# Layer 1 attention of a two-layer MoE transformer: first loads, norms, and the turning of attention outputs rearranged

## The chip, the cores and the metric

The kernel runs on one core of a Trainium2 chip. The metric is device time in microseconds (us) of one execution; lower is better. The time of the kernel before is the median of three runs. A profile is one further execution, taken by the hardware profiler; its times count from the start of its span.

## The reference, cut to what matters

A two-layer transformer works on 1024 image tokens and 256 context tokens of width 1024. Each layer normalises its tokens (RMS norm, then scale and shift from a conditioning vector), attends, projects back, adds the result, normalises again, routes every token to 2 of 32 experts and adds the experts' outputs. Layer 1 is sliding-window attention with 16 heads of 64, 4 key/value heads, and a "sink" logit per head:

```python
h = _modulate(_rmsnorm(x, norm1_g[i]), sh1, sc1)
hc = _modulate(_rmsnorm(xc, norm1_g[i]), shc1, scc1)
...
q, k = _rope(q, cos, sin), _rope(k, cos, sin)
...
p = softmax(concat([q k / sqrt(d) + mask, sink]))[..., :-1]
o = p v
x = x + g1 * (o @ w_o)
```

The RMS norm is `x * rsqrt(mean(x*x) + 1e-6)`. Before layer 1, its input is the sum of layer 0's residual and of the two weighted expert outputs of each token, times a gate row (`g2`).

## The kernel before, in words

Everything is float32 in precision: an operand of a large matmul is split into a high and a low part, and two or three matmuls make one product. The stages follow one another: attention 0, projection and routing of layer 0, 32 experts, attention 1, projection and routing of layer 1, 32 experts, a last norm.

Tokens come in 10 tiles of 128: tiles 0 to 7 are the image, 8 and 9 the context. `attention1` (from L1377) takes them in the order 8, 9, 0, 1, ... and has a generator `tick` (L1457) that runs four things for four tiles at once: `combine` of a tile (L1345, ScalarE scales one expert row; L1346, VectorE adds the other; L1348, times `g2`, on VectorE for the first four tiles and on GpSimd for the rest; L1349 adds the residual), `norm1_a` of the tile before (L280: squares with a row sum on ScalarE, `rsqrt`, then the scaled copy L287 on VectorE), `norm1_b` of the tile before that (L290: eight transposes on TensorE, L298; scale and shift of the first four 128-column pieces on ScalarE, L304, of the last four on VectorE, L306; L308 and L309 split into high and low), and the loads of a later tile. `combine_load` (L1341) loads two expert rows per token (`c_y`, L1329) and, for tiles that are not there already, the residual (`c_x`, L1336). `c_y` has four buffers, so the fifth `c_y` load waits until `combine` has released one.

`rsqrt` (L261) is one helper for every norm of the kernel: 10 norms at the start of attention 0, 10 with eight columns (L772) and 18 with one column (L845) in the two projection stages, 10 in attention 1, 8 in the last norm. It computes `v = ss*scale + eps` on VectorE (L268, or L270 where `add` is given), the root on ScalarE (L271), the reciprocal (L272) and one Newton step in four VectorE operations (L273 to L276).

The main loop has four groups of heads. In step `s` of a group it projects the next tile (`qkv`, L337), rotates and transposes queries and keys (L1425, L1432), makes scores (L1539, L1540), and exponentials (L1546 on VectorE, L1555 on ScalarE), and turns the probabilities (L1493) to multiply them with the values (L1504, L1505). A value tile holds high parts in columns 0 to 63 and low parts in columns 64 to 127, so `oT` holds, for 4 heads x 128 queries, 64 rows from the high parts and 64 from the low. `last` (L1510) ends one block (one of 4 groups, one of 8 query tiles; 32 in all): four matmuls (L1515) with a 128x64 matrix `I2`, two stacked identities, turn the block and add its two halves; VectorE multiplies by the reciprocal sums (L1517); ScalarE's queue issues the store (L1518).

```python
pt = ps_t.tile([P, 4, P], F32, name="tr")
for i in range(4):
    nc.tensor.matmul(pt[:, i, 0:64], st["ot"][:, i * P:(i + 1) * P], I2, start=True, stop=True)
oc = pl.tile([P, 4, 64], F32, name="oc", bufs=2)
nc.vector.tensor_tensor(oc, pt[:, :, 0:64], bc(rr, 64, 2), op=OP.mult)
...
```

All transposes and these matmuls write to one ring of two PSUM buffers (`tr`). Every engine and every queue works its instructions in order; which order that is, the framework's scheduler settles when the kernel is built, from the program's order and from what it expects to be ready. So the order in a trace can differ from the text (the small `sink` load stands ahead of the second half of a tile's `c_y` loads, for example). During groups 0 to 2 a second generator, `gen_mods` (L203), makes the conditioning rows of layer 1 with ScalarE (L224) and GpSimd (L225 to L230) beside the rest.

Of the kernel before, what the change touches and what calls it, by code (L numbers as in the profile page):

```python
# [17 lines left out]
OP = mybir.AluOpType  # L18
# [76 lines left out]
class Kernel:  # L95
# [165 lines left out]
    def rsqrt(self, ss, scale, pool, add=None):  # L261

        nc = self.nc
        n = ss.shape[1]
        w = pool.tile([P, 4, n], F32, name=f"rsq{n}", bufs=2)
        v, r, t = w[:, 0, :], w[:, 1, :], w[:, 2, :]
        if add is None:
            nc.vector.tensor_scalar(v, ss, scale, EPS, op0=OP.mult, op1=OP.add)  # L268
        else:
            nc.vector.scalar_tensor_tensor(v, ss, scale, add, op0=OP.mult, op1=OP.add)  # L270
        nc.scalar.activation(t, v, AF.Sqrt)  # L271
        nc.vector.reciprocal(r, t)  # L272
        nc.vector.tensor_tensor(t, r, r, op=OP.mult)  # L273
        nc.vector.tensor_tensor(t, t, v, op=OP.mult)  # L274
        nc.vector.tensor_scalar(t, t, -0.5, 1.5, op0=OP.mult, op1=OP.add)  # L275
        nc.vector.tensor_tensor(w[:, 3, :], r, t, op=OP.mult)  # L276
        return w[:, 3, :]


    def norm1_a(self, xt, pool):  # L280

        nc = self.nc
        xn = pool.tile([P, D], F32, name="n1_xn", bufs=2)
        ss = pool.tile([P, 1], F32, name="n1_ss", bufs=2)
        nc.scalar.activation(xn, xt, AF.Square, accum_out=ss)
        rs = self.rsqrt(ss, 1.0 / D, pool)
        nc.vector.tensor_scalar(xn, xt, rs, None, op0=OP.mult)  # L287
        return xn

    def norm1_b(self, l, t, xn, pool, trp, hT):  # L290

        nc = self.nc
        v = 0 if t < NX else 1
        for half in range(2):
# [5 lines left out]
            for q in range(4):  # L300
                k = half * 4 + q
                a, b = self.Acol[l][:, k, v:v + 1], self.Bcol[l][:, k, v:v + 1]
                if half == 0:
                    nc.scalar.activation(hf[:, q, :], pt[:, q, :], AF.Identity, bias=b, scale=a)  # L304
# [1066 lines left out]
    def attention1(self, es_wo, es_raw, es_o, es2):  # L1371
# [5 lines left out]
        with ExitStack() as es:  # L1377
# [21 lines left out]
            mask = mask.rearrange("p a b -> p (a b)")  # L1399
            I2 = pk.tile([P, 64], F32, name="I2")  # L1400
            nc.vector.tensor_tensor(I2, self.ident[:, 0:64], self.ident[:, 64:P], op=OP.add)

# [42 lines left out]
            work = [[8, 9, 0]] + [[t] for t in range(1, NX)]  # L1445
            g2 = lambda v: self.row_tile(pre, f"g2_{v}", self.mods[0][v:v + 1, 5 * D:6 * D], tag="g2", bufs=2)
            g2 = {1: g2(1), 0: g2(0)}
            prep_w(0)
            while parts:
                parts.popleft()()  # L1450
            ld = {t: self.combine_load(0, t, pre, 2) for t in order[:3]}
            sk = self.row_tile(pk, "sink", A["b_sink"].rearrange("(o d) -> o d", o=1))
# [5 lines left out]
            def tick(i):  # L1458
# [8 lines left out]
                if 0 <= i + 2 < NT:  # L1467
                    xn[order[i + 2]] = self.norm1_a(xs.pop(order[i + 2]), pre)
                yield
                if 0 <= i + 1 < NT:  # L1470
                    t = order[i + 1]
                    hTn[t] = (pa, pre)[(i + 1) % 3 // 2].tile([P, 2, KC, P], F32R, name="hT", bufs=2 - (i + 1) % 3 // 2)
                    self.norm1_b(1, t, xn.pop(t), pre, ps_t, hTn[t])
                yield
# [10 lines left out]
            def av(g, b, E, rr, keys):  # L1485
# [24 lines left out]
                def last():  # L1510
# [3 lines left out]
                    for i in range(4):  # L1514
                        nc.tensor.matmul(pt[:, i, 0:64], st["ot"][:, i * P:(i + 1) * P], I2, start=True, stop=True)  # L1515
                    oc = pl.tile([P, 4, 64], F32, name="oc", bufs=2)
                    nc.vector.tensor_tensor(oc, pt[:, :, 0:64], bc(rr, 64, 2), op=OP.mult)  # L1517
                    getattr(nc, STQ['os1']).dma_start(self.os[b * P:(b + 1) * P, g * 256:(g + 1) * 256].rearrange(  # L1518
# [241 lines left out]
```

## Time and profile before

| | |
|---|---|
| median of 3 runs (lowest, highest) | 3034.24 us (3033.3, 3034.73) |
| the profiled execution, time | 3037.21 us |
| the profiled execution, span | 3035.4 us |
| mean granted clock of TensorE | 0.961 of full speed |

The span is divided as the trace's windows divide it: attention 0 up to about 900 us, projection 0 to about 1085, experts 0 to about 1673, attention 1 to about 2300 (its last steps share time with projection 1, to about 2400), experts 1 to 2987, the last norm to the end. A row of the window view gives the busy time of each engine in a stretch; a row of a line or of a tile gives how often an instruction ran and its shortest, median and longest time in ns; a timeline row gives a start, a length, and in brackets how long the engine was idle before and what released it.

### The profile page before, as it was taken

To read this page: it belongs to the slowest core of one execution; us is meant where nothing else is said; L and a number is where in the kernel's file an instruction comes from. 1 tells how busy PE (TensorE), PEld (TensorE's weight loads), DVE (VectorE), ACT (ScalarE), POOL (GpSimd) and SP (SyncE) were. 2 spreads that over 40 slices of the span, in tenths; PEclk is the share of its full clock that TensorE was granted. 3 is DMA by queue.
4 is the path that set the end of the run, shared out by engine and by line. 5 is a ranking of instruction groups with operands and counts; after the bars stand their busy time and mean duration, and the time that the engine had idled before them with its cause. 6 is when DMAs were issued, how large, how long until landed. Compare 5 with 4: busy or idle time off the path is not lost. (4 is left out here: it accounts for less than half of the span.)

```text
span 3035.4 us, 44263 instructions
## 1 busy us (share of the span) xinstructions
PE 2783.7 (92%) x15206; PEld 2349.0 (77%) x15206; DVE 2422.0 (80%) x4162; ACT 2096.9 (69%) x3725; POOL 1052.7 (35%) x887
## 2 busy tenths in 40 slices
PE   7999999999979979999999489998999799999992
PEld 3888888888857768888888478887888677777772
DVE  4778777777778879989998686665666699999997
ACT  5777777777753258888888487876553478888783
POOL 4756665665521111111110344655100133333330
PEclk8999999999989989999999699999999899999996
DMA  7644554444325479999999745444236799999996
GB/s 259 232 165 165 176 176 161 166 163 157 128 103 202 138 275 377 380 379 377 377 376 352 276 167 180 162 145 153 94 105 212 255 347 365 373 371 368 336 368 265
DMA packets 303214, 745.52 MB, mean 246 GB/s; under 512 B 24612, under 2 KB 80520, under 8 KB 287624
## 3 DMA queue, kind: packets, MB, share of 16 engines
q1 hardware_dynamic: 265032, 680.72, 62.6%
q0 software_dynamic: 19584, 41.98, 3.7%
q10 hardware_dynamic: 18368, 19.93, 1.9%
q8 instruction: 122, 2.00, 0.3%
q14 instruction: 108, 0.88, 0.1%
HBM read 680.60 MB, written 91.29 MB: 254 GB/s over the span
## 5 line engine op out<-in xcount | busy, mean ns | idle before, releaser
L1092 DVE TENSOR_TENSOR elo<-wr,ehi 128x1024 fp32r<-128x1024 f32 x768 | 948.6, 1288 | 62.2 <-ACT ehi L1090 62.2
L1090 ACT ACTIVATE ehi<-wr 128x1024 fp32r<-128x1024 f32 x768 | 762.8, 1061 | 3.3 <-PE y L1158 1.5
L337 PE MATMUL qkv<-w_hi,hT 128*128 128x384 f32 (+1 forms) x1920 | 543.8, 351 | 14.6 <-ACT hT L308 4.9
L337 PEld LDWEIGHTS qkv<-w_hi,hT 128*128 128x128 f32 x1920 | 353.2, 196 | 32.4 <-issue 14.4
L337 PE MATMUL qkv<-w_lo,hT 128*128 128x384 f32 (+1 forms) x960 | 334.3, 348 | 0.0
L1158 PE MATMUL y<-ehi,hidT 128*128 128x512 f32 x1024 | 317.8, 392 | 4.2 <-DVE yb L1169 3.0
L1144 PE MATMUL pg<-ehi,xT 128*128 128x512 f32 x1024 | 291.9, 407 | 3.3 <-ACT ehi L1090 3.3
L1144 PE MATMUL pu<-ehi,xT 128*128 128x512 f32 x1024 | 281.0, 396 | 0.0
L1119 POOL DMA_INDIRECT y_s<-yb,dI x64 | 77.2, 1206 | 513.8 <-ACT yb L1171 482.7
L586 DVE TENSOR_SCALAR_CACHE_REDUCE E<-S 128x1280 f32<-128x1280 f32 (+1 forms) x160 | 203.5, 1272 | 60.8 <-PE S L603 58.8
L1158 PEld LDWEIGHTS y<-ehi,hidT 128*128 128x128 f32 x1024 | 192.5, 188 | 45.7 <-issue 3.4
L594 ACT ACTIVATE E<-E,mx 128x1280 f32<-128x1280 f32 (+1 forms) x160 | 190.9, 1193 | 49.0 <-DVE E L586 48.3
L1173 POOL TENSOR_TENSOR yb<-yb,g 128x1024 f32<-128x1024 f32 x30 | 86.9, 2898 | 374.5 <-ACT yb L1171 374.5
L1144 PEld LDWEIGHTS pu<-ehi,xT 128*128 128x128 f32 x1024 | 187.8, 188 | 36.7
L1144 PEld LDWEIGHTS pg<-ehi,xT 128*128 128x128 f32 x1024 | 184.8, 191 | 37.4 <-ACT ehi L1090 4.1
L1158 PE MATMUL y<-elo,hidT 128*128 128x512 f32 x512 | 200.3, 391 | 0.1
L337 PEld LDWEIGHTS qkv<-w_lo,hT 128*128 128x128 f32 x960 | 187.7, 196 | 5.8 <-issue 4.3
L224 ACT ACTIVATE mpr<-mraw,sf 128x256 f32<-128x256 f32 x320 | 145.3, 504 | 29.1 <-POOL macc L227 21.4
L1144 PE MATMUL pg<-elo,xT 128*128 128x512 f32 x512 | 163.1, 400 | 2.2
L601 PE MATMUL S<-K,Qh 128*128 128x512 f32 (+1 forms) x416 | 152.9, 368 | 13.1 <-DVE E L586 13.1
L1144 PE MATMUL pu<-elo,xT 128*128 128x512 f32 x512 | 160.7, 395 | 0.1
L361 POOL TENSOR_TENSOR rd<-rp_a,rp_u 128x256 f32<-128x256 f32 (+1 forms) x96 | 89.9, 937 | 198.1 <-DVE rp_u L356 87.5
(294 smaller groups left out, 6637.8 us busy)
## 6 DMA issues: line engine op xcount, KB each, us to landing
wr<-in_wg SPq DMA_DIRECT2D x128, 1024.0 KB
wr<-in_wu SPq DMA_DIRECT2D x128, 1024.0 KB
wr<-in_wd SPq DMA_DIRECT2D x128, 1024.0 KB
hT<-hTs SPq DMA_DIRECT2D x100, 1024.0 KB
mraw<-in_mod_w SPq DMA_DIRECT2D x80, 512.0 KB
hTs<-hT SPq DMA_DIRECT2D x20, 1024.0 KB
c_y<-y_s SPq DMA_DIRECT2D x36, 512.0 KB
w_raw<-in_a_qkv SPq DMA_DIRECT2D x32, 384.0 KB
```

The lines of the kernel that those rows point to most:

```text
L224: nc.scalar.activation(pr[v][:, q], raw[:, q], AF.Copy, scale=self.sf[:, 4 * i + q, v:v + 1])
L337: self.nc.tensor.matmul(ps[:, 0:n], hT[:, a, k, :], W[b][:, k, c0:c0 + n], start=(i == 0), stop=(i == 3 * KC - 1))
L361: nc.gpsimd.tensor_tensor(rd[:, :, 0, :], av, uu, op=OP.add)
L586: nc.vector.tensor_scalar(E[:, 0:n], Sf[:, 0:n], -0.125, None, op0=OP.mult, op1=OP.min, accum_out=mx)
L594: nc.scalar.activation(E[:, 0:n], E[:, 0:n], AF.Exp, bias=mx, scale=-1.0, accum_out=acc)
L601: nc.tensor.matmul(Sf[:, n0:n0 + w], Qh[:, m, j * P:(j + 1) * P], K[h][:, m, o:o + w], start=True, stop=False)
L1090: nc.scalar.activation(hi, raw, AF.Copy)
L1092: nc.vector.tensor_tensor(lo[:, 0:c], raw[:, 0:c], hi[:, 0:c].bitcast(F32), op=OP.subtract)
L1119: nc.gpsimd.indirect_dma_start(out=self.ybs[l], out_offset=bass.IndirectOffsetOnAxis(ap=idx, axis=0), in_=yb, in_offset=None, bounds_check ...
L1144: nc.tensor.matmul(o, xt[:, a, k, :], w[:, q * 512:(q + 1) * 512], start=(k == 0 and a == 0 and w is hi), stop=(k == KC - 1 and w is lo))
L1158: nc.tensor.matmul(y[:, half, :], hT[:, a, k, :], w[:, f], start=(k == 0 and a == 0 and w is hi), stop=(k == 3 and w is lo))
L1173: nc.gpsimd.tensor_tensor(yb, yb, g2, op=OP.mult)
```

## The change

Four edits, all in one kernel.

1. `rsqrt`: where there is no `add`, ScalarE takes the root straight from the row sum, with scale and eps inside its instruction; VectorE makes `v = -0.5*(ss*scale + eps)` beside it. The Newton step becomes two operations after the reciprocal for one column, three for eight columns.
2. `attention1`: the first loads are issued in another order (the `c_y` of tile 8, its gate row, the `c_y` of tile 9, of tile 0, the other gate row), and a one-element root is taken on ScalarE ahead of them.
3. The scaled copy of `norm1_a` goes to ScalarE for the first five tiles, and six of the eight pieces of `norm1_b` instead of four for the first four tiles.
4. `last`: four plain transposes with the identity instead of matmuls with `I2`. ScalarE copies the low halves out of PSUM, VectorE adds the high halves, GpSimd multiplies by the reciprocal sums. `I2` goes.

```diff
         if add is None:
-            nc.vector.tensor_scalar(v, ss, scale, EPS, op0=OP.mult, op1=OP.add)
+            nc.scalar.activation(t, ss, AF.Sqrt, bias=self.eps, scale=scale)
+            nc.vector.tensor_scalar(v, ss, -0.5 * scale, -0.5 * EPS, op0=OP.mult, op1=OP.add)
         else:
             nc.vector.scalar_tensor_tensor(v, ss, scale, add, op0=OP.mult, op1=OP.add)
-        nc.scalar.activation(t, v, AF.Sqrt)
+            nc.scalar.activation(t, v, AF.Sqrt)
+            nc.vector.tensor_scalar(v, v, -0.5, None, op0=OP.mult)
         nc.vector.reciprocal(r, t)
-        nc.vector.tensor_tensor(t, r, r, op=OP.mult)
-        nc.vector.tensor_tensor(t, t, v, op=OP.mult)
-        nc.vector.tensor_scalar(t, t, -0.5, 1.5, op0=OP.mult, op1=OP.add)
-        nc.vector.tensor_tensor(w[:, 3, :], r, t, op=OP.mult)
+        if n == 1:
+            nc.vector.scalar_tensor_tensor(t, r, v, r, op0=OP.mult, op1=OP.mult)
+        else:
+            nc.vector.tensor_tensor(t, v, r, op=OP.mult)
+            nc.vector.tensor_tensor(t, t, r, op=OP.mult)
+        nc.vector.scalar_tensor_tensor(w[:, 3, :], t, 1.5, r, op0=OP.add, op1=OP.mult)
...
-    def norm1_a(self, xt, pool):
+    def norm1_a(self, xt, pool, act=False):
...
-        nc.vector.tensor_scalar(xn, xt, rs, None, op0=OP.mult)
+        if act:
+            nc.scalar.activation(xn, xt, AF.Copy, scale=rs)
+        else:
+            nc.vector.tensor_scalar(xn, xt, rs, None, op0=OP.mult)
...
-    def norm1_b(self, l, t, xn, pool, trp, hT):
+    def norm1_b(self, l, t, xn, pool, trp, hT, act=4):
...
-                if half == 0:
+                if k < act:
                     nc.scalar.activation(hf[:, q, :], pt[:, q, :], AF.Identity, bias=b, scale=a)
...
-            I2 = pk.tile([P, 64], F32, name="I2")
-            nc.vector.tensor_tensor(I2, self.ident[:, 0:64], self.ident[:, 64:P], op=OP.add)
...
-            g2 = lambda v: self.row_tile(pre, f"g2_{v}", self.mods[0][v:v + 1, 5 * D:6 * D], tag="g2", bufs=2)
-            g2 = {1: g2(1), 0: g2(0)}
             prep_w(0)
             while parts:
                 parts.popleft()()
-            ld = {t: self.combine_load(0, t, pre, 2) for t in order[:3]}
+
+            nc.scalar.activation(pk.tile([P, 1], F32, name="root"), self.eps, AF.Sqrt)
+            g2, ld = {}, {}
+            for t in order[:3]:
+                ld[t] = self.combine_load(0, t, pre, 2)
+                if t != 9:
+                    v = 1 if t == 8 else 0
+                    g2[v] = self.row_tile(pre, f"g2_{v}", self.mods[0][v:v + 1, 5 * D:6 * D], tag="g2", bufs=2)
...
-                    xn[order[i + 2]] = self.norm1_a(xs.pop(order[i + 2]), pre)
+                    xn[order[i + 2]] = self.norm1_a(xs.pop(order[i + 2]), pre, i + 2 < 5)
...
-                    self.norm1_b(1, t, xn.pop(t), pre, ps_t, hTn[t])
+                    self.norm1_b(1, t, xn.pop(t), pre, ps_t, hTn[t], 6 if i + 1 < 4 else 4)
...
-                        nc.tensor.matmul(pt[:, i, 0:64], st["ot"][:, i * P:(i + 1) * P], I2, start=True, stop=True)
+                        nc.tensor.transpose(pt[:, i, :], st["ot"][:, i * P:(i + 1) * P], self.ident)
+
                     oc = pl.tile([P, 4, 64], F32, name="oc", bufs=2)
-                    nc.vector.tensor_tensor(oc, pt[:, :, 0:64], bc(rr, 64, 2), op=OP.mult)
+                    nc.scalar.activation(oc, pt[:, :, 64:P], AF.Copy)
+                    nc.vector.tensor_tensor(oc, pt[:, :, 0:64], oc, op=OP.add)
+                    nc.gpsimd.tensor_tensor(oc, oc, bc(rr, 64, 2), op=OP.mult)
```

## Rows read from the trace of the kernel before

**Rows 1.** Windows: stretch; us; busy us of PE, PEld, DVE, ACT, POOL; clock; DMA share; GB/s
```profile
1701.00:1735.00 34.00, 24.13 (x116) 22.28 (x117) 31.39 (x58) 21.01 (x48) 20.66 (x14) 0.63 0.89 315
...
2000.00:2100.00 100.00, 93.02 (x602) 79.58 (x600) 65.84 (x156) 74.64 (x181) 55.53 (x55) 0.99 0.38 131
2100.00:2200.00 100.00, 96.78 (x628) 87.11 (x628) 61.93 (x155) 53.12 (x126) 21.38 (x18) 0.98 0.34 120
```

**Rows 2.** Timeline of SP's queue (start, length, line) at the head of attention 1
```profile
1682.30 0.80 SPq L691 DMA_DIRECT2D g<-mod_s  x2
1683.15 10.04 SPq L1329 DMA_DIRECT2D c_y<-y_s  x5
```

**Rows 3.** Timeline, ScalarE, VectorE and TensorE: from the first loads to the next table load
```profile
1690.19 1.15 ACT L1345 ACTIVATE c_y<-c_y,wts 128x1024 f32<-128x1024 f32 x1 [8.18 <-DMA c_y<-y_s]
1691.56 1.28 DVE L1346 SCALAR_TENSOR_TENSOR c_y<-c_y,wts,c_y 128x1024 f32<-128x1024 f32 x1 [8.46 <-DMA c_y<-y_s]
...
1696.36 0.19 ACT L285 ACTIVATION_READ_ACCUMULATOR n_xn<-xg 128x1 f32 x1
...
1698.10 1.28 ACT L271 ACT_TABLE_LOAD   x1
...
1700.60 0.75 DVE L287 TENSOR_SCALAR n_xn<-xg,rsq 128x1024 f32<-128x1024 f32 x1
...
1701.40 1.97 PE L298 MATMUL tr<-ident,n_xn 128*128 128x128 f32 x8 [28.56 <-DMA c_y<-y_s]
...
1759.29 1.28 ACT L1555 ACT_TABLE_LOAD   x1
```

**Rows 4.** Tile `rsq`, 1690 to 1800 us: count, ns shortest/median/longest
```profile
L287 DVE TENSOR_SCALAR n_xn<-xg,rsq x3: 752/1753/1761, 1700.6 to 1715.2; 128x1024 f32<-128x1024 f32 x3
```

**Rows 5.** Lines L304 and L306, 1690 to 1820 us: count, ns shortest/median/longest
```profile
L304 ACT ACTIVATE n_hf<-tr,Bcol,Acol x40: 441/457/483, 1703.5 to 1812.8; 128x128 f32<-128x128 f32 x40
L306 DVE TENSOR_SCALAR n_hf<-tr,Acol,Bcol x40: 392/402/410, 1703.8 to 1814.4; 128x128 f32<-128x128 f32 x40
```

**Rows 6.** Timeline of PE: one block's end, the matmul after it, eight transposes
```profile
2059.35 1.10 PE L1515 MATMUL tr<-I,ot 128*128 128x64 f32 x8
2060.26 0.31 PE L1540 MATMUL S<-K,Q 128*128 128x128 f32 x1
...
2061.32 0.60 PE L1493 MATMUL tr<-ident,E 128*128 128x128 f32 x4
2061.76 0.60 PE L1425 MATMUL tr<-ident,rd 128*128 128x128 f32 x4
```

**Rows 7.** Tile `oc`, whole span: count, ns shortest/median/longest, first and last start
```profile
L1517 DVE TENSOR_TENSOR oc<-tr,acc x32: 415/425/426, 1792.0 to 2297.7; 128x256 f32<-128x256 f32 x32
```

**Rows 8.** Lines by form: count; busy us, mean ns; idle us before and releaser
```profile
L468 ACT ACTIVATE Qh<-tr 128x256 fp32r<-128x256 f32 x72 | 27.5, 382 | 10.7 <-PE tr L466 9.7
L227 POOL TENSOR_TENSOR macc<-mpr 128x256 f32<-128x256 f32 x12 | 8.9, 738 | 33.1 <-DMA mod_s<-macc 33.0
```

**Rows 9.** Waits, 1800 to 2300 us: who waited for whom; us in total, times, longest
```profile
ACT h L844 <- DVE oc L1517: 2.0, 1, 2.0
...
ACT mpr L224 <- DVE oc L1517: 0.4, 1, 0.4
```

**Rows 10.** Timeline of VectorE and TensorE in the norms of attention 0
```profile
58.14 1.57 DVE L273 TENSOR_TENSOR rsq<-rsq 128x1 f32<-128x1 f32 x1
...
64.51 1.11 PE L298 MATMUL tr<-ident,n_xn 128*128 128x128 f32 x4 [4.16 <-DVE n_xn L287]
```

**Rows 11.** Timeline of VectorE: the end of the span
```profile
3029.60 0.15 DVE L272 RECIPROCAL rsq<-rsq 128x1 f32<-128x1 f32 x1
...
3030.56 1.29 DVE L1367 SCALAR_TENSOR_TENSOR o<-wr,rsq,fg 128x1024 f32<-128x1024 f32 x1
```

**Rows 12.** Timeline of VectorE and POOL: a one-column product beside a GpSimd product
```profile
1718.26 2.36 POOL L1348 TENSOR_TENSOR c_y<-c_y,g 128x1024 f32<-128x1024 f32 x1 [1.17 <-DVE rsq L268]
1718.70 1.94 DVE L273 TENSOR_TENSOR rsq<-rsq 128x1 f32<-128x1 f32 x1
```

## The prediction, made before the changed kernel ran

> **What bounds the kernel now.** I read the page's slices first, for where TensorE is not full, then the windows of attention 1, then the queue and the engines at its head, then the waits for what the change touches, and last the end of the span. Three regions matter.
>
> In the main loop of attention 1 TensorE is the bound: busy 93.0 and 96.8 of 100 us in two windows, with VectorE at 62 to 66 and ScalarE at 53 to 75 [rows 1]. What is taken off TensorE there comes off the time, if nothing new makes it wait.
>
> At the head of attention 1 TensorE has nothing to do until the first norm: it starts its transposes at 1701.40 after 28.56 us idle [rows 3]. The chain before is loads, then small steps. After it VectorE is the bound, busy 31.4 of 34 us from 1701 to 1735, and ScalarE only 21.0 [rows 1].
>
> At the end of the span VectorE alone decides, working through the last norms to the last product [rows 11].
>
> **The change, part by part.** The sum is made against the profiled execution, 3037.2 us (span 3035.4). The median of the runs is 3.0 lower, so the sum's result is shifted by 3.0.
>
> *First loads.* SP issues two gate rows, then the expert rows from 1683.15; the fourth transfer is used at 1691.56 [rows 2, 3]. Four transfers in 9.3 us make 2.3 each, issue and start included. Afterwards the pair of tile 8 is first and second instead of third and fourth: at most 4.6 us earlier, at least the 0.8 of issue time. The gate row now comes third and is wanted 1.28 (L1346) after the second: it is about 1.0 late. I take 3.6. The other gate row falls behind the loads of tile 0, which wait for released buffers; tile 0's product comes two combines later, which hides it, and without that cover it costs one transfer, 2.3. The sink and residual loads behind it on SP are wanted later still. The root load, the missing `I2` and GpSimd's queue cost nothing here: ScalarE and VectorE stand idle for 8 us before the first expert row, and GpSimd until the first split.
>
> *Root and Newton step.* From the end of the row sum (1696.36 + 0.19) to the scaled copy (1700.60) pass 4.05 us [rows 3]. The table load, 1.28, moves ahead to ScalarE's idle time. VectorE's first small step leaves the chain, and of five steps after the root three stay: at the end of the span five take 0.96 from start to next [rows 11], so 0.19 each, 0.4 for two and about 0.3 for the first. Against that, the copy on ScalarE takes as long as L1345, 1.15 instead of 0.75. Gain 1.28 + 0.7 - 0.4 = 1.6, with 0 and 2.5 as ends: nothing if VectorE's queue holds the three steps as long as the five, and more if it no longer holds the root.
>
> *Work moved to ScalarE.* In 1701 to 1735 fall about four of the five copies: VectorE loses 4 x 1.25 (0.75 to 1.76 [rows 4]), 6 pieces of 0.40 and four times two small steps, 8.6 in all, and goes to about 22.8. ScalarE gains 4 x 1.15 and 6 x 0.46 [rows 5], 7.4, and goes to 28.4. The fuller engine goes from 31.4 to 28.4: at most 3.0 gained, at least 0, since the other is late next. I take 1.0.
>
> *Turning the outputs.* From the start of the eight `I2` passes to the next matmul are 0.91 us; from four transposes to the next ones 0.44 [rows 6]. TensorE gives back 0.47 per block, 15.0 over 32 blocks [rows 7]. Added: a ScalarE copy out of PSUM, 0.38 like L468, 12.2 in all, and a GpSimd product, 0.74 like L227, 23.6 in all [rows 8]; VectorE's addition takes the place of a product of the same shape (0.42). The PSUM buffer is held about 0.6 longer (copy and handover), and the store is ready about 1.5 later: copy, product, two handovers of 0.2. The store's issue stands on ScalarE's queue, and whatever comes behind it there (copies of probabilities, exponentials, `gen_mods`) waits too; before, there were 3.6 us of such waits, in four of 32 blocks (three rows, the first and the last in [rows 9]). So the gain lies between 15.0 and 0 if all is hidden or all of it turns into waits. ScalarE has 25 of 100 us idle and VectorE 34 [rows 1], nearer to hidden: I take a third as lost, 10.0 kept.
>
> *The root helper elsewhere.* In attention 0, TensorE waits 4.16 for a scaled copy behind a one-column product that took 1.57 [rows 10]; one such product is gone. Gain 0 to 4, taken 1.5. In the last norm VectorE drops two small steps for each of eight tiles, at 0.07 between large ones to 0.16 alone: 1.1 to 2.6, taken 1.8. In the projections TensorE or the loads lead; 0 taken, 1 at most. With eight columns the count of steps stays.
>
> Sum: 3.6 + 1.6 + 1.0 + 10.0 + 1.5 + 1.8 = 19.5. 3037.2 - 19.5 = 3017.7, as a median 3014.7. All upper ends (4.6, 2.5, 3.0, 15.0, 4, 2.6, 1) make 32.7 and 3001.5; all lower ends (0.8, 0, 0, 0, 0, 1.1, 0) 1.9 and 3032.3.
>
> **The rivals.**
>
> *A: the new eviction takes the loop's gain.* The two PSUM buffers are held 0.6 longer, and TensorE waits for a buffer where it used to multiply. For it: 0.6 is more than the 0.47 saved. Against it: scores and projections, which need no such buffer, follow the block's end [rows 6]. The main loop gives 0, the rest 9.5: 3024.7.
>
> *B: slower, through the store on ScalarE's queue.* ScalarE stands at the store's issue until GpSimd has multiplied, and GpSimd may itself stand before an L227 that waits for a transfer (33.0 us over 12 [rows 8]). If each block's 1.5 us pass to TensorE whole, 48 are lost against 24.5 gained without loss (15.0 + 9.5): 23.5 slower, 3057.7. It decides from 0.77 us per block; at 1.0 the time is 3041.7. Against it: ScalarE's idle quarter is some 4 us per block of 16 us [rows 1, 7], and a scheduler can put other work ahead of the store.
>
> *C: ScalarE becomes the bound at the head.* Seven more microseconds on it, in order, undo what the loads and the root bring; front 0, the rest 13.3: 3020.9.
>
> *D: GpSimd's products hold VectorE.* A one-column product that otherwise takes 0.16 took 1.94 and ended with GpSimd's product [rows 12]. 32 new products of 0.74 are 23.6 us in which VectorE operations with two SBUF operands would stand. Most of VectorE's work in the loop reads PSUM; if every second product passes its length on to TensorE, 11.8 are lost: 3026.5. The Trainium skill, page "SBUF — State Buffer", section "SBUF: two separate sides", states that VectorE and GpSimd share a port pair under an exclusive lock, kept for the whole instruction. By that rule, which these rows fit, moving a product to GpSimd has a price that its own length doesn't show.
>
> *E: the early root does not do what it is for.* Another function set is loaded between it and the first norm; 1.3 comes back: 3016.0. Against it: after the load at 1698.10 the next one comes at 1759.29, for an exponential; copies, squares and scalings between them need none [rows 3].
>
> **How the numbers follow.** Forecast 0.44, A 0.18, B 0.10, C 0.13, D 0.10, E 0.05. The range takes in A, C, D, E and the bounds, and leaves out B and the far ends: 3003 to 3033. A difference under 0.2%, 6.1 us, cannot be told from none here. Faster by more (below 3028.2): nearly all of the forecast (0.42), A 0.11, C 0.11, D 0.06, E 0.05, together 0.75. Within it: 0.02 of the forecast, A 0.06, C 0.02, D 0.04, together 0.14. Slower: B 0.10 and 0.01 of A, 0.11.
>
> **What would show it.** The first transposes of attention 1 about 5 us earlier after the loop's end, with a Sqrt table load in ScalarE's idle time and none in front of the first root; ScalarE the fullest engine until about 1735; four transposes in place of eight passes, 0.45 to the next matmul; main loop shorter by about 10 us; last norm shorter by nearly 2. Wrong would be: TensorE's idle time in the main loop grown by 10 us or more, with waits for the new copy, sum or product in front of it, or ScalarE standing behind the store for over a microsecond per block (B); VectorE's small steps stretched by GpSimd (D); or a head that ends no earlier at 1735 though its loads land earlier (C).

## The result, and the profile after

The changed kernel is slower: 3054.35 us (median of 7 executions, 3044.39 to 3057.18) against 3033.51 (7 executions beside them). The ratio is 1.0064, 95% interval 1.0053 to 1.0075. The prediction said 3014.7. The profiled execution took 3055.27 us with a span of 3053.4, 18.0 longer than the span before.

**Where the 18.0 us lie.** Four marks divide the span: the end of the last matmul of the first experts, the start of VectorE's `oc` operation in the first and in the last of the 32 blocks ([rows 7] before), and the end. All are read from timelines.

| | to the experts' end | experts' end to first block | first to last block | last block to end |
|---|---|---|---|---|
| before | 1672.9 | 119.1 | 505.7 | 737.7 |
| after | 1675.7 | 125.0 | 518.8 | 733.9 |
| difference | +2.8 | +5.8 | +13.2 | -3.8 |

The first column can't be told from noise: single executions of kernels whose instructions are alike up to there differ by more (1668.6 with the new turning of outputs alone, which leaves everything before attention 1 as it was). The same kernel, whose head is that of the kernel before too, reaches its first block 124.7 us after the experts, so the 5.8 of the second column can't be laid on the edits at the head by this table alone; the experiments have to show it. The loss is in attention 1, and most of it in the main loop.

**The stretches of [rows 1] after** (windows; columns as there):

```profile
1701.00:1735.00 34.00, 19.80 (x88) 18.25 (x87) 19.80 (x37) 27.22 (x60) 19.29 (x15) 0.55 0.93 335
1703.80:1737.80 34.00, 21.86 (x100) 20.72 (x101) 18.18 (x35) 25.95 (x58) 20.81 (x14) 0.59 0.94 341
...
2000.00:2100.00 100.00, 92.66 (x577) 76.96 (x576) 67.81 (x158) 79.32 (x199) 60.63 (x69) 1.00 0.37 127
2100.00:2200.00 100.00, 92.33 (x578) 83.13 (x578) 59.22 (x149) 58.57 (x136) 32.74 (x26) 0.93 0.38 134
```

At the head the work did move: VectorE 31.39 to 19.80 us, ScalarE 21.01 to 27.22. But TensorE does less in the same 34 us, 19.80 instead of 24.13 (21.86 in the second row, which lies as far behind the experts' end as the stretch before did). In the loop TensorE should be full with less to do; instead it idles more in the last stretch (92.33 for 96.78). These two stretches are fixed times, in which the changed kernel is some 18 to 21 us behind, so they hold other blocks; the whole loop follows below.

**The head, answering [rows 2, 3]** (timeline of the changed kernel: SP's queue, ScalarE, VectorE, GpSimd, TensorE):

```profile
1682.69 1.28 ACT L1456 ACT_TABLE_LOAD   x1 [4.46 <-SPq L1274]
...
1683.83 0.81 SPq L1337 DMA_DIRECT2D c_y<-y_s  x2
...
1694.39 0.19 ACT L289 ACTIVATION_READ_ACCUMULATOR n_xn<-xg 128x1 f32 x1
1694.61 0.29 ACT L268 ACTIVATE rsq<-n_ss,eps 128x1 f32<-128x1 f32 x1
1694.94 0.16 DVE L274 RECIPROCAL rsq<-rsq 128x1 f32<-128x1 f32 x1
1695.02 1.21 DVE L1356 TENSOR_TENSOR c_y<-c_y,g 128x1024 f32<-128x1024 f32 x1
1696.14 0.21 DVE L276 SCALAR_TENSOR_TENSOR rsq<-rsq 128x1 f32<-128x1 f32 x1
1696.27 1.22 DVE L1357 TENSOR_TENSOR xg<-xg,c_y 128x1024 f32<-128x1024 f32 x1
1697.41 0.15 DVE L280 SCALAR_TENSOR_TENSOR rsq<-rsq 128x1 f32<-128x1 f32 x1
...
1698.58 1.13 ACT L292 ACTIVATE n_xn<-xg,rsq 128x1024 f32<-128x1024 f32 x1
1699.77 1.97 PE L306 MATMUL tr<-ident,n_xn 128*128 128x128 f32 x8 [24.12 <-ACT n_xn L292]
...
1704.87 1.12 PE L306 MATMUL tr<-ident,n_xn 128*128 128x128 f32 x4 [3.13 <-ACT n_hf L312]
...
1721.58 2.33 POOL L1356 TENSOR_TENSOR c_y<-c_y,g 128x1024 f32<-128x1024 f32 x1
1721.66 2.27 DVE L280 SCALAR_TENSOR_TENSOR rsq<-rsq 128x1 f32<-128x1 f32 x1
...
1723.96 1.15 ACT L292 ACTIVATE n_xn<-c_x,rsq 128x1024 f32<-128x1024 f32 x1 [4.26 <-DVE rsq L280]
...
1725.16 1.12 PE L306 MATMUL tr<-ident,n_xn 128*128 128x128 f32 x4 [5.83 <-ACT n_xn L292]
```

The table load sits in ScalarE's idle time and none stands before the first root. TensorE's first transposes come 24.1 us after the experts instead of 28.6 (27.5 to 28.6 in the eight kernels with the old loads and the old first root), so 4.4 of the 5.2 us promised (3.6 + 1.6) came. They all came from the loads: the row sum ends 18.9 us after the experts instead of 23.7. From the row sum (1694.58) to the copy (1698.58) pass 4.00 us, as before (4.05), although the table load is gone and the steps are fewer: between the reciprocal and the last step VectorE puts two operations of tile 9, 1.2 us each, and the copy stands behind tile 9's square on ScalarE. Then the lead is lost: TensorE waits 3.13 us for a piece that ScalarE is late with, later 5.83 for a scaled copy (the last rows: the last Newton step is held 2.27 us beside a GpSimd product, and the copy on ScalarE waits 4.26 for it), and the first projection with 384 columns starts 56.0 us after the experts (1731.68) instead of 52.5 (1725.32).

**The turning of outputs, answering [rows 6, 7, 8]** (timeline of TensorE at one block's end; then tile `oc`: count, ns shortest/median/longest):

```profile
2079.84 0.66 PE L1526 MATMUL tr<-ident,ot 128*128 128x128 f32 x4 [0.16 <-ACT ot L1519]
2080.25 0.42 PE L345 MATMUL qkv<-w_hi,hT 128*128 128x384 f32 x1
```

```profile
L1529 ACT ACTIVATE oc<-tr x32: 362/384/389, 1800.1 to 2319.0; 128x256 f32<-128x256 f32 x32
L1530 DVE TENSOR_TENSOR oc<-tr,oc x32: 411/424/426, 1800.6 to 2319.5; 128x256 f32<-128x256 f32 x32
L1531 POOL TENSOR_TENSOR oc<-oc,acc x32: 609/615/938, 1801.1 to 2320.0; 128x256 f32<-128x256 f32 x32
```

0.41 us from the transposes to the next matmul (0.44 was taken), a copy of 0.38 (0.38), a product of 0.62 (0.74): every price was about right. What goes wrong stands between them. One block, in time order (timelines of the changed kernel):

```profile
1883.44 1.30 POOL L225 TENSOR_TENSOR mpr<-mpr 128x512 f32<-128x512 f32 x1
1883.75 0.42 DVE L1530 TENSOR_TENSOR oc<-tr,oc 128x256 f32<-128x256 f32 x1 [0.84 <-ACT oc L1529]
1884.82 0.73 POOL L229 TENSOR_TENSOR mpr<-mpr 128x256 f32<-128x256 f32 x1
1885.62 0.74 POOL L230 TENSOR_TENSOR macc<-macc,mpr 128x256 f32<-128x256 f32 x1
1886.32 0.61 POOL L1531 TENSOR_TENSOR oc<-oc,acc 128x256 f32<-128x256 f32 x1
1886.96 0.33 ACTq L1532 DMA_DIRECT2D o_s<-oc  x1
1887.34 0.72 ACT L1569 ACTIVATE E<-E,mx 128x512 f32<-128x512 f32 x1 [2.82 <-POOL oc L1531]
...
1889.37 0.69 DVE L1508 TENSOR_TENSOR aT<-tr,aT 128x512 fp32r<-128x512 f32 x1 [3.85 <-ACT aT L1507]
...
1890.12 0.47 PE L1438 MATMUL tr<-ident,rd 128*128 128x128 f32 x1 [2.96 <-DVE aT L1508]
```

The addition is done at 1884.17. GpSimd is working on the conditioning rows of `gen_mods` and multiplies 2.2 us later; ScalarE stands at the store; the exponential behind it starts 2.82 late; the copy of probabilities behind that, VectorE's subtraction (3.85) and TensorE (2.96) follow. Six of the 32 products start 2.0 to 3.6 us after their addition starts, the others after 0.5 to 0.65. In all six GpSimd is not waiting but busy: with products of `gen_mods` and rotations in five, with a split of projection weights (L721) in the sixth. What ScalarE waited for (waits, 1790 to 2340 us: us in total, times, longest), where [rows 9] had 3.6 us:

```profile
ACT E L1569 <- POOL oc L1531: 13.7, 6, 3.1
...
ACT Q L1433 <- POOL oc L1531: 2.2, 1, 2.2
...
ACT aT L1507 <- POOL oc L1531: 1.7, 1, 1.7
```

With two more of 1.0 and 0.9 these are 19.5 us. The wait costs more than its length, because TensorE comes back from it at a lower granted clock (windows of the changed kernel before, in and after that pause; the clock stands before the last two columns):

```profile
1870.00:1883.00 13.00, 12.41 (x75) 9.73 (x76) 8.91 (x21) 9.45 (x26) 3.83 (x6) 1.00 0.23 77
1887.00:1890.00 3.00, 0.16 (x2) 0.02 (x1) 0.63 (x2) 2.66 (x7) 2.61 (x3) 0.82 0.12 44
1890.00:1896.00 6.00, 5.88 (x17) 3.70 (x17) 3.58 (x9) 4.47 (x13) 1.28 (x1) 0.52 0.29 91
```

0.52 is the level of 1.2 GHz. In those 6 us TensorE is busy 5.88 with 17 matmuls; in the 13 before, 75 took 12.41.

**The small ends, answering [rows 10, 11].** In attention 0 the last scores start at 887.8, before at 888.9. That shows no gain: the seven kernels of this document with the old helper there have them between 885.0 and 888.9, the ten with the new one between 884.6 and 888.2. At the end of the span (timeline of the changed kernel, VectorE) two steps follow the reciprocal:

```profile
3046.49 0.16 DVE L274 RECIPROCAL rsq<-rsq 128x1 f32<-128x1 f32 x1
...
3046.69 0.22 DVE L276 SCALAR_TENSOR_TENSOR rsq<-rsq 128x1 f32<-128x1 f32 x1
...
3048.02 0.15 DVE L280 SCALAR_TENSOR_TENSOR rsq<-rsq 128x1 f32<-128x1 f32 x1
3048.21 1.28 DVE L1375 SCALAR_TENSOR_TENSOR o<-wr,rsq,fg 128x1024 f32<-128x1024 f32 x1
```

From the end of the last matmul of the second experts to the end are 48.7 us, 50.2 before: 1.4 gained. Here the helper's gain is seen each time: 48.1 to 48.7 in the ten kernels that have it, 49.8 to 50.8 in the seven without.

### The profile page after: what moved, and what is told of

Its sections match the earlier page's. It is cut to its first block, busy times and chain, and to the rows that moved or that the text cites. A ratio compares the mean times of both kernels' runs of the same rounds, so it can differ in the third digit from the quotient of the medians.

```text
span 3053.4 us, 44053 instructions
## 1 busy us (share of the span) xinstructions
PE 2788.5 (91%) x15078; PEld 2348.2 (77%) x15078; DVE 2403.0 (79%) x4056; ACT 2118.6 (69%) x3771; POOL 1070.8 (35%) x919
## 5 line engine op out<-in xcount | busy, mean ns | idle before, releaser
L345 PE MATMUL qkv<-w_hi,hT 128*128 128x384 f32 (+1 forms) x1920 | 551.0, 355 | 18.1 <-DMA hT<-hTs 8.9
L345 PEld LDWEIGHTS qkv<-w_hi,hT 128*128 128x128 f32 x1920 | 360.0, 199 | 34.7 <-issue 13.8
L602 ACT ACTIVATE E<-E,mx 128x1280 f32<-128x1280 f32 (+1 forms) x160 | 190.9, 1193 | 51.2 <-DVE E L594 50.2
L1137 ACT ACTIVATE xT<-tr 128x512 fp32r<-128x512 f32 x128 | 76.7, 600 | 115.2 <-PE tr L1133 115.2
```

The costliest lines, as they stand in the source:

```text
L345: self.nc.tensor.matmul(ps[:, 0:n], hT[:, a, k, :], W[b][:, k, c0:c0 + n], start=(i == 0), stop=(i == 3 * KC - 1))
L602: nc.scalar.activation(E[:, 0:n], E[:, 0:n], AF.Exp, bias=mx, scale=-1.0, accum_out=acc)
L1137: nc.scalar.activation(dst[:, 0], pt, AF.Copy)
```

## The experiments

Fifteen kernels, each timed in turns with the kernel before on one chip (5 to 12 executions each, 29 or 35 of the kernel before in each of four series). A ratio is to the kernel before of its series, with its 95% interval. Theory Store: ScalarE stands at the store behind GpSimd. Theory Head: the loss begins with the norms.

**Turning alone.** The kernel before with edit 4 as it stands in the diff, nothing else.

```diff
-    nc.tensor.matmul(pt[:, i, 0:64], st["ot"][:, i * P:(i + 1) * P], I2, start=True, stop=True)
-nc.vector.tensor_tensor(oc, pt[:, :, 0:64], bc(rr, 64, 2), op=OP.mult)
+    nc.tensor.transpose(pt[:, i, :], st["ot"][:, i * P:(i + 1) * P], self.ident)
+nc.scalar.activation(oc, pt[:, :, 64:P], AF.Copy)
+nc.vector.tensor_tensor(oc, pt[:, :, 0:64], oc, op=OP.add)
+nc.gpsimd.tensor_tensor(oc, oc, bc(rr, 64, 2), op=OP.mult)
```

> The kernel before with the new turning of outputs alone (edit 4); rsqrt, loads and norms are the old ones. Measured against the kernel before, 3033.5 us. Theory Store (ScalarE stands at the store until GpSimd has multiplied): in the changed kernel ScalarE waited 18.5 us for GpSimd's product (13.7 + 2.2 + 1.7 + 0.9 us in the wait view) and the blocks fell 12 us further behind between the 1st and the 12th; this edit alone gives 3042 to 3048, with 10 us or more of ScalarE waits for GpSimd's product. Theory Head (the loss comes from the norms and the first loads, and the loop only carries it on): this edit alone gives 3018 to 3034. The prediction's step (10.0 kept) would be 3023.5.

1.0047 (1.0032 to 1.0062), 3045.40 us for 3032.82. The turning alone costs some 14 us, in Store's range and far from the 10 us of gain that the prediction took. ScalarE waits 19.4 us for GpSimd's product in its profile.

**All but the turning.** The changed kernel with that diff the other way round, and `I2`.

> The changed kernel with the old turning of outputs (eight I2 passes, VectorE's product); edits 1 to 3 stay. Theory Store: what is left of the loss is what the profile shows at the first block, 8.6 us behind, less 1.4 in the last norm: 3038 to 3042. Theory Head: the whole loss stays, 3050 to 3056. The prediction's steps (9.5 us gained by edits 1 to 3) would be 3024.

1.0018 (1.0007 to 1.0030), 3039.75 us. Edits 1 to 3 together cost some 5 us, inside Store's range. Head's 3050 is out; so is the prediction's 3024.

**The store on GpSimd's queue.**

```diff
-STQ = dict(..., os1='scalar', ...)
+STQ = dict(..., os1='gpsimd', ...)
```

> The changed kernel with the attention output's store issued by GpSimd's queue, right behind GpSimd's own product, instead of ScalarE's. Theory Store: ScalarE's waits for GpSimd's product (18.5 us) go to zero and the 12 us lost in the loop come back: 3040 to 3045; GpSimd pays 32 issues of about 0.6 us, which it has idle. Theory Ring (the PSUM buffer held longer by the copy and the handover makes TensorE wait): unchanged, 3052 to 3057, and TensorE's idle time stays in front of the transposes. Theory Head: unchanged too.

1.0010 (0.9999 to 1.0021), 3034.21 us: 20 us less than the changed kernel by the medians, 16 by the ratios, by one word, and more than theory Store had asked for. ScalarE's waits that end with this tile go from 19.5 us to 2.2. First to last block took 498.0 us instead of 518.8 (windows; the changed kernel, then this one):

```profile
1800.63:2319.46 518.83, 477.50 (x2916) 408.15 (x2915) 333.38 (x798) 353.20 (x839) 203.50 (x217) 0.96 0.38 133
```

```profile
1800.32:2298.28 497.96, 464.03 (x2915) 398.24 (x2914) 332.85 (x798) 353.18 (x839) 219.73 (x248) 0.98 0.40 139
```

TensorE runs as many matmuls in both, but for one. Of the 20.9 us, 7.4 are idle time of TensorE and 13.5 are matmuls that took longer, at a mean clock of 0.96 instead of 0.98: the larger part of the price is paid behind the waits, not in them. In the Trainium skill, page "DMA: Bandwidth & Descriptors", section "Anatomy of one DMA — SWDGE (gpsimd) path", it stands that a transfer's wait for a semaphore happens on the issuing sequencer, before dispatch. The 2.82 us at 1887.34 and this run fit that.

**The product on VectorE.**

```diff
-nc.gpsimd.tensor_tensor(oc, oc, bc(rr, 64, 2), op=OP.mult)
+nc.vector.tensor_tensor(oc, oc, bc(rr, 64, 2), op=OP.mult)
```

> The changed kernel with the product by the reciprocal sums on VectorE, right behind its addition, instead of GpSimd; the store stays on ScalarE's queue. Theory Store: GpSimd's own queue (products of the conditioning rows and rotations ahead of the product, 2.6 us in the block at 1883.7) is what makes the wait long; with VectorE the store is ready some 0.5 us after the addition, ScalarE's waits at the store shrink from 18.5 to under 6 us, and 3042 to 3047 result. Theory Ring: unchanged, 3052 to 3057. If VectorE becomes late instead (32 more products of 0.3 to 0.4 us, 12 us on an engine that is busy 62 to 66 of 100 us), the time stays above 3050 with TensorE waiting for VectorE's subtraction.

0.9989 (0.9979 to 0.9998), 3030.61 us. The store stays on ScalarE's queue; only GpSimd's place between addition and store is gone, and 24 us with it (23 by the ratios), again more than Store had asked for. Its bound for ScalarE's waits (under 6) was missed: they are 7.0. Ring falls with both runs, and so does the fear of a late VectorE.

**The same with nothing else changed.** Edit 4 with the product on VectorE, in the kernel before: the first diff above, its last line being

```diff
+nc.vector.tensor_tensor(oc, oc, bc(rr, 64, 2), op=OP.mult)
```

> The kernel before with the new turning of outputs, but the product on VectorE right behind its addition; nothing else is changed. Theory Store: without GpSimd's queue in front of the store the four transposes bring what the prediction took for them, 8 to 11 us: 3022 to 3025, and ScalarE's waits for the stored tile are under 8 us instead of 19. If the gain of the product on VectorE in the run with edits 1 to 3 came from elsewhere (their norms), this kernel stays at 3030 to 3034.

0.9985 (0.9976 to 0.9994), 3028.28 us: a gain, but 4 to 5 us, not 8 to 11. The loop shows why (windows from the first to the last block; first the kernel before, then turning alone with GpSimd's product, then this one):

```profile
1791.99:2297.66 505.67, 481.70 (x3044) 418.92 (x3043) 333.35 (x806) 343.13 (x807) 184.90 (x186) 0.97 0.39 137
```

```profile
1793.32:2305.71 512.39, 471.49 (x2912) 402.91 (x2912) 331.29 (x799) 351.18 (x836) 204.01 (x217) 0.97 0.39 135
```

```profile
1790.97:2291.15 500.18, 465.31 (x2914) 401.19 (x2913) 347.27 (x830) 352.34 (x836) 185.19 (x186) 0.98 0.40 138
```

TensorE is busy 16.4 us less (481.70 to 465.31), as the 15.0 of the prediction said. Its idle time grows from 24.0 to 34.9, so 5.5 are kept of 16.4 in this profile. The figure is rough: from the first to the last block the five profiles with VectorE's product and ScalarE's store take 498 to 504 us, and with the old turning seven of eight take 502 to 506. With GpSimd's product TensorE's idle time grows to 40.9, while only 10.2 busy us go. What is late next is a transfer (waits of TensorE, 1791 to 2305 us, this kernel):

```profile
PE qkv L337 <- DMA hT<-hTs: 8.4, 3, 4.8
PE tr L1430 <- DVE aT L1495: 8.0, 6, 4.5
PE tr L1513 <- ACT ot L1506: 7.5, 15, 1.8
```

The kernel before waited 0.2 us for the reload of `hT`, and 4.2 for the copy `ot`. These two grew by 11.5 us, the idle time by 10.9; no run takes them away, so that they are the cause is not shown. The expectation's bound for ScalarE's waits at the store (under 8) was missed: they are 9.0, half of them in two waits of a norm of the next stage.

**The helper alone** (edit 1).

```diff
-nc.vector.tensor_scalar(v, ss, scale, EPS, op0=OP.mult, op1=OP.add)
-nc.scalar.activation(t, v, AF.Sqrt)
+nc.scalar.activation(t, ss, AF.Sqrt, bias=self.eps, scale=scale)
+nc.vector.tensor_scalar(v, ss, -0.5 * scale, -0.5 * EPS, op0=OP.mult, op1=OP.add)
...
```

> The kernel before with the new rsqrt helper alone (edit 1). The prediction's steps for it: 1.5 us in attention 0, 1.8 in the last norm, 0.7 in the first norm of attention 1: 3028 to 3029.5 against 3033. The traces so far: from VectorE's last block to the end the changed kernel needs 733.9 us, the kernel before 737.7, so that 1.8 is seen or more. Rival (the steps left are still queued between VectorE's 1.2 us operations, as at 1694.94 to 1697.41 in the changed kernel, where three steps took 2.6 us): no gain at the head, 3031 to 3033.

1.0008 (0.9997 to 1.0019), 3034.99 us for 3032.15. The first transposes come 26.9 us after the experts (28.6 before), but 1.2 of that is a row sum that ends earlier, which the edit doesn't touch; from the row sum to the copy pass 3.59 us instead of 4.05. No gain reaches the end: the prediction's steps for it are missed, and the time is at or just above the rival's.

**First loads and early root alone** (edit 2).

```diff
-ld = {t: self.combine_load(0, t, pre, 2) for t in order[:3]}
+nc.scalar.activation(pk.tile([P, 1], F32, name="root"), self.eps, AF.Sqrt)
+for t in order[:3]:
+    ld[t] = self.combine_load(0, t, pre, 2)
...
```

> The kernel before with the new order of the first loads and the early root alone (edit 2). Measured from the last matmul of the experts, the first transposes of attention 1 came after 28.55 us before and after 24.1 to 24.9 in the four kernels that have edits 1 to 3. Theory Front (edit 2 brings these 4.4 us, and they reach the end): first transposes after 25 to 26 us, 3028 to 3030. Rival Given back (the gate row of tile 0, now behind the first expert rows, and VectorE's full queue until 1735 use it up): first transposes as early, first 384-column projection no earlier than the 52.5 us after the experts of the kernel before, 3032 to 3035.

1.0016 (1.0006 to 1.0026), 3036.26 us. The row sum ends 19.4 us after the experts (23.7 before), the first transposes start at 26.9, the first 384-column projection at 52.0 (52.5 before): Given back, as far as the place goes, and then a loss of some 5 us, which neither theory had. Most of the lead is gone before the first transposes: from the row sum to the copy pass 6.67 us instead of 4.05, because with the rows there earlier VectorE has operations of 1.2 us of the next tiles between the five small steps.

**Norms on ScalarE alone** (edit 3).

```diff
-self.norm1_a(xs.pop(order[i + 2]), pre)
+self.norm1_a(xs.pop(order[i + 2]), pre, i + 2 < 5)
...
-self.norm1_b(1, t, xn.pop(t), pre, ps_t, hTn[t])
+self.norm1_b(1, t, xn.pop(t), pre, ps_t, hTn[t], 6 if i + 1 < 4 else 4)
```

> The kernel before with the work moved to ScalarE alone (edit 3). The prediction's step is a gain of 1.0 with 0 to 3.0 as ends: 3030 to 3033. Theory ScalarE (in the changed kernel the second half of a norm's pieces stands behind a scaled copy and a scaled expert row of later tiles on ScalarE, TensorE waits 3.1 us for a piece and 5.8 for a scaled copy, and the first 384-column projection comes 56.0 us after the experts instead of 52.5): from the first transposes to that projection 7 to 8 us longer than in the kernel before (23.9 us), and 3037 to 3042.

1.0055 (1.0042 to 1.0068), 3049.09 us for 3032.15. This is the dearest edit, and it costs about twice the upper end of what theory ScalarE expected. The first 384-column projection starts 62.2 us after the experts, 9.7 later than before, and the first block 16 later; from the first to the last block the loop takes 503.8, nothing more. The profile shows a wait where the prediction saw a load (timeline of this kernel, GpSimd, VectorE, ScalarE, TensorE):

```profile
1711.63 2.35 POOL L1351 TENSOR_TENSOR c_y<-c_y,g 128x1024 f32<-128x1024 f32 x1 [1.17 <-DVE rsq L272]
1711.66 2.33 DVE L273 TENSOR_TENSOR rsq<-rsq 128x1 f32<-128x1 f32 x1
...
1714.66 1.15 ACT L288 ACTIVATE n_xn<-xg,rsq 128x1024 f32<-128x1024 f32 x1 [3.84 <-DVE rsq L276]
1715.72 0.61 ACT L311 ACTIVATE hT<-n_hf 128x512 fp32r<-128x512 f32 x1
1716.39 0.48 PE L340 MATMUL qkv<-w_hi,hT 128*128 128x128 f32 x1 [3.48 <-ACT hT L311]
```

The scaled copy stands on ScalarE and waits for VectorE's Newton step. The step that should take 0.16 us is held 2.33 beside GpSimd's product, as in [rows 12]. The split of the tile before (L311) had its operands, but stands behind the copy, and TensorE waits 3.48 for it. When the copy was VectorE's, no split stood behind it. From 1672 to 1830 TensorE waits 9.6 us for ScalarE's splits, 3.0 in the kernel before. The Trainium skill, page "Perfetto Trace Analysis", section "Tensor Engine Instruction (MATMUL, LD_WEIGHTS)", says in an aside that ScalarE, VectorE and GpSimd work as strict queues; these five rows fit.

**One half of edit 3: the copies**, the first pair of lines of this diff.

> The kernel before with one half of edit 3: the scaled copies of the first five norms on ScalarE, the pieces shared four and four as before. Edit 3 whole cost 16.9 us. Theory Queue (a copy is one link of the chain root, Newton step, copy, transposes, and on ScalarE it stands behind squares and scaled expert rows of 1.1 us each of later tiles): this half carries most of it, 3043 to 3048. Theory Load (ScalarE is simply given too much, 4.6 us of copies and 2.8 of pieces in 34 us): it carries about six tenths, 3042 to 3044. Rival Pieces (the second half of a tile's pieces has to wait for ScalarE before its split): little, 3033 to 3037.

1.0015 (1.0002 to 1.0029), 3039.20 us for 3034.36. **The other half: six pieces of eight**, the second pair.

> The kernel before with the other half of edit 3: six of eight pieces of the first four norms on ScalarE, the scaled copies on VectorE as before. Theory Queue: little, 3033 to 3037. Theory Load: about four tenths of 16.9 us, 3038 to 3041. Rival Pieces: most of it, 3043 to 3048. The two halves need not add up to the whole, since every edit gives the engines another order of their instructions.

1.0028 (1.0016 to 1.0041), 3044.33 us for 3034.36. My theory Queue falls in the form in which I put it: the copies are not most of it, the pieces cost at least as much. Load and Pieces don't give both halves either. The halves are 4.3 thousandths together, the whole 5.5. In the half with the pieces TensorE waits 6.1 and 7.4 us for the splits of ScalarE and GpSimd from 1672 to 1830; the kernel before, 3.0 and 3.4. But the half with the copies shows as much (6.9 and 6.6) and costs less, and the profile of the pieces, the longest of its 12 executions, has its first 384-column projection no later than before (51.5) and its main loop 8.8 us longer. That the pieces cost is measured; by what way is not shown.

**The parts put together.** Edits 1, 2 and 4 with the product on VectorE, without edit 3.

```diff
-self.norm1_a(xs.pop(order[i + 2]), pre, i + 2 < 5)
+self.norm1_a(xs.pop(order[i + 2]), pre)
...
-nc.gpsimd.tensor_tensor(oc, oc, bc(rr, 64, 2), op=OP.mult)
+nc.vector.tensor_tensor(oc, oc, bc(rr, 64, 2), op=OP.mult)
```

> Edits 1, 2 and 4 with the product on VectorE; edit 3 left out. If the parts add up against 3032: +2.8 and +4.1 for edits 1 and 2, -3.9 for the turning: 3035. If the gains that each edit shows at its place (first transposes 4.4 us earlier, last norm 1.4 shorter, turning 9) reach the end once edit 3 doesn't hold the head: 3019 to 3024. With edit 3 the same kernel took 3030.6.

0.9976 (0.9964 to 0.9988), 3029.59 us for 3034.36: the fastest of the series, some 7 us below the kernel before, less than the places promise and more than the single edits add up to. By its interval it is not told apart from the turning with VectorE's product alone (0.9985). **Edits 1 and 4 with the product on VectorE**, loads and root of the kernel before as well.

> Edits 1 and 4 with the product on VectorE. The turning with the product on VectorE alone took 3028.3. If edit 1 brings in the last norm and in attention 0 what the prediction took (1.8 and 1.5) and the head is not disturbed: 3024 to 3026. If edit 1 costs as much at the head as it did alone (first block 4.7 us later after the experts, 2.8 us in all): 3029 to 3032.

0.9986 (0.9974 to 0.9999), 3032.18 us for 3034.36: no different from the turning with VectorE's product alone.

**The helper everywhere but in attention 1's norms.** `rsqrt_old` is the helper before.

```diff
-self.norm1_a(xs.pop(order[i + 2]), pre)
+self.norm1_a(xs.pop(order[i + 2]), pre, True)
...
-rs = self.rsqrt(ss, 1.0 / D, pool)
+rs = (self.rsqrt_old if old else self.rsqrt)(ss, 1.0 / D, pool)
```

> The kernel before with the new rsqrt helper in attention 0, the projections and the last norm, and the old one in the norms of attention 1, whose instructions keep the order of the kernel before there (on TensorE 3593 of 3631 up to the next experts). With the new helper everywhere TensorE's order in attention 1 differs from the 12th instruction on, and 2.8 us were lost. Theory Order (that loss is the other order of the work at the head of attention 1, not the helper): the prediction's steps for attention 0 and the last norm come through, 1.5 + 1.8: 3029 to 3032 against some 3033, faster by 1.5 to 4. Rival Helper (the new steps themselves cost, or bring nothing anywhere): 3033 to 3037.

1.0003 (0.9992 to 1.0013), 3033.53 us for 3034.52. Order is not borne out: a gain of over 2.4 us is outside the interval. The last norm is 2.1 us shorter at its place (48.1 for 50.2); so small a gain these intervals can't tell from none. **With the turning and VectorE's product.**

> The same helper choice, and the new turning with the product on VectorE; loads and norms of attention 1 as before. Theory Order: what the turning with the product on VectorE brought alone (0.15 per cent, some 4 us) and the helper elsewhere (1.5 to 4) add up, 3024 to 3028. Rival Helper: 3028 to 3033.

0.9982 (0.9972 to 0.9993), 3027.36 us for 3034.52: inside the figure that Order had set, but by its ratio no different from the turning with VectorE's product alone, so it settles nothing between the two.

**The parts put together, with the store on GpSimd's queue**, by the one-word diff above.

> Edits 1, 2 and 4 with the product on VectorE, and the store on GpSimd's queue in place of ScalarE's; edit 3 left out. With the store on ScalarE's queue this kernel took 0.24 per cent less than the kernel before. If what is left of ScalarE's waits at the store (7 us in the run with edits 1 to 3) reaches TensorE: 3 to 6 us faster than that, 0.35 to 0.45 per cent below the kernel before. If those waits are hidden, no change, or up to 3 us slower, because GpSimd now stands at the store until VectorE has multiplied and its rotations of queries and keys come later.

1.0003 (0.9991 to 1.0015), 3034.26 us: some 8 us slower than with ScalarE's queue (each by its ratio to the kernel before of its own series). Once VectorE makes the product, the store is better left where it was, in this kernel. Its profiled execution was among its shortest (span 3025.4) and doesn't show the loss, so the reason stays open.

## Why the prediction was wrong, point by point

- **What bounds the kernel** was right: TensorE in the loop, the first norms at the head.
- **Turning the outputs** (10.0 kept of 15.0, ends 15.0 and 0) is the first step that failed. TensorE's saving was right (16.4 in the run with VectorE's product). The failure is "I take a third as lost", with zero as the lower end: the range supposed that the added waits can at most eat the gain. As written, edit 4 costs some 14 us alone. The prediction's own sign came: TensorE's idle time in the loop grew by 17.4 us (24.0 to 41.3). Rival B named the place, ScalarE standing at the store, and it is shown by two runs that take it away in different ways, 20 and 24 us below the changed kernel (16 and 23 by the ratios). B's reason for a late GpSimd was another: it had GpSimd waiting for a transfer, and in the six late blocks GpSimd is busy. B's threshold didn't hold either: ScalarE's waits are 0.6 us per block on average, below B's 0.77, but they come as few waits of 2 to 3 us, TensorE pays the pause and then matmuls at the lower clock, and the 9.5 us that B set against them from the other edits were not there. It also needs an average over blocks that are unlike: `gen_mods` fills GpSimd's queue in some of them only. My argument against B, an idle quarter of ScalarE, counts nothing in an engine that works in order.
- **Even without that wait** some 5.5 us of the loop's 16.4 are kept where 10.0 were taken; the reload of `hT` (8.4 us) is the longest new wait, and the prediction did not name it.
- **Work moved to ScalarE** (1.0, ends 0 and 3.0) is the second step that failed. VectorE's and ScalarE's busy times came out near the forecast (19.8 for 22.8; 27.2 for 28.4), and that said nothing: the edit alone costs some 17 us. Rival C had the engine right but the wrong reason (it is full) and too low a price, the gain of the front at most. For the copies the rows show another: a step of a chain was put on an engine with other tiles' work behind it, and a wait for the chain now holds that work. How much of the 17 us that is, no run shows, and for the pieces, the half that costs at least as much, the way stays open.
- **First loads** (3.6) were a little undersized at their place: the row sum ends 4.8 earlier, just above the upper end of 4.6, and 4.3 with edit 2 alone. But that kernel lost some 5 us. The prediction took a gain at the front for one at the end; part of it goes into VectorE's queue at once, and before the first 384-column projection it is gone.
- **Root and Newton chain** (1.6): nothing in the changed kernel, its lower end, and for the reason named there, VectorE's queue; 0.5 with edit 1 alone. Rival E did not happen.
- **Helper elsewhere**: 1.4 in the last norm (1.8 taken), at its place; nothing that can be told from noise in attention 0 (1.5 taken). A kernel with just these shows no gain in its time.
- **D** happened at the head, as rows that existed before had shown, and lay in the chain that the moved copy waits for. In the loop the 32 new products are not seen to hold VectorE: its subtraction of probabilities (688 ns) and its masked minimum (879 ns) keep their means; both take an operand from PSUM, so they say little on the operations that D feared for. **A** was not it: no wait of TensorE for the new copy's buffer is among its longest.

Left open: why edit 2 alone ends at a loss; why the pieces of edit 3 cost what they do; why edits 1 and 2 take back two thirds of what edit 3 costs alone (1.0055 alone, 1.0018 with them); and how much of either is the other order which the framework's scheduler gives to the whole stage after any edit at its head. The run meant to tell that (the helper everywhere but in attention 1) gave no difference either way. The turning alone and its version with VectorE's product have the same order of instructions up to the first block, yet their profiles reach it 124.7 and 120.2 us after the experts; a single profile can't settle a few microseconds there.

## What to carry to other kernels

Before work is moved to another engine, ask of each moved instruction whose result it waits for and what stands behind it in the new queue; a store's issue counts as such an instruction. An idle share of the engine is no cover for a wait, and the lower end of such an edit lies below nothing. Keep producer and consumer of a short chain on one engine where you can, and keep work that arrives in bursts (here `gen_mods` on GpSimd) out of a chain that TensorE ends up waiting for.

## What the runs showed of the hardware that was not expected

- A pause of TensorE of 2.96 us was followed by 6 us at a granted clock of 0.52, with a pair of the 384-column matmuls at 0.84 us where it takes 0.51 at full clock, so the pause cost about as much again behind it (an estimate: 0.48 of 6 us is 2.9).
- The fused steps of the helper are longer than the plain ones: the root with scale and eps inside takes 0.29 us (0.20 before, medians), the product of three 0.22 (0.16). Two steps fewer save less than two steps' time.
- A VectorE step on 128 single elements takes 2.33 us beside a GpSimd product of 2.35 that starts 0.03 before it.
